# Attention's transposed probabilities returned in chunks of four key blocks, and each half's scores issued ahead of the other half's products with v

## The chip, the cores and the metric

The kernel runs on one core of a Trainium2 chip. The time is the device time of one launch in microseconds, as the median of several runs. TensorE (PE) multiplies matrices, with its weight loads shown apart (PEld); VectorE (DVE), ScalarE (ACT) and GpSimd (POOL) work on elements; SyncE (SP) issues all DMAs of this kernel in one queue, in order.

## The reference

One layer of a decoder on 2048 positions of width 1024, in float32: a mixer with three groups of heads (a Mamba-2 SSD, an RG-LRU and a forgetting attention), a SwiGLU feed-forward of width 2816, and a gated projection of a second input p, each added to the residual stream behind an RMS norm. The part that matters here is the forgetting attention: six heads of 64, in blocks of 128 queries.

```
cum = cumsum(log_f)
for blk in range(s // 128):
    logits = (q[blk] . k[:q1]) * scale + cum[queries] - cum[keys]
    probs = softmax(where(causal, logits, -inf))
    out[blk] = probs . v[:q1]
```

and behind it

```
h = h + concat[ssd, lru, fox] @ w_out
u = rmsnorm(h);  h = h + (silu(u @ w_gate) * (u @ w_up)) @ w_down
u = rmsnorm(h);  h = h + sigmoid(u @ w_ple_gate + b) * (p @ w_ple_proj)
```

## The kernel before

Activations lie transposed: 128 channels on the partitions, 512 positions (a block, four of them) in the free dimension. Every large product is made of float32r halves: a number is split into a rounded part and a rest, and three matmuls (high x high, high x low, low x high) are summed in PSUM. `mm3` (L194) makes one such product of a 128-column slab of weights: 8 x 3 matmuls of 512 columns. Its weights are loaded to `wst` (two buffers, L184), ScalarE copies the rounded part to `w` (three buffers, L190) and GpSimd subtracts it (L191).

The kernel has three phases. The first two make q, k, v, the recurrences and the SSD, and attention for block 0 (by another routine, `attention`). `phase3` (L802) then goes through the four blocks: gate and up products in three groups of hidden slabs with the down products behind each group (`FSPLIT`), then the projection of p and its gate, then `finish`, and in between the mixing product (`mix`, `load_y`) of the next block.

While block tb runs its feed-forward, attention for block tb + 1 runs at the side: `attention_t` (L692) is a Python generator, and `Side.tick` (L55) draws from it. Each `mm3` adds `rate` to a credit, and each whole credit runs the generator to its next `yield`. The rate is set so that all yields of a block are spent over RATE = 45 products. A last call, `side.finish()` in `load_y`, draws whatever is left, ahead of the norm of attention's output (L784 to L788).

This fixes the order in which the program is traced. A planner then takes all traced instructions, gives each the priority of its place in the program, and writes each engine's queue in a simulation of its own: an engine takes the first instruction in program order that the simulation believes ready, so a later one can be put ahead of an earlier one that waits. On the chip each engine works through its written queue in order, and semaphores hold it where data or buffers are late.

In `attention_t` for block qc there are K = 4 (qc + 1) key blocks, six heads, and per head two halves of 256 queries, hv = 1 and hv = 0. Per head k goes to `kx`, the forget bias to `cum`, q to `qx` and `qh`, v to `vc`, each with one buffer. For each 128-query block of a half, four score matmul pairs (L730, L731) are made, one per group of 32 keys out of each key block, with a yield behind each; VectorE adds the bias and takes the maximum (L732, into `lg`, two buffers); ScalarE takes the exponential with its sum (L738) and scales (L741); VectorE transposes squares of 32 x 32 (L742). Four DMAs write the result to a DRAM scratch `dp` (L746), and one reads it back with keys on the partitions into `pT` (L747). `pT` holds both query blocks of a half over all its key blocks, and has one buffer. When both are there (four empty yields, GAP, stand in between), `pT` is split into halves `ph` (two buffers): ScalarE copies the rounded part (L757), VectorE or GpSimd in turn subtracts (L758), and two matmuls per key block multiply with v into the PSUM bank `xd` (L761, L762), with a yield per key block. A copy (L765), an addition and a DMA to `dy` end the half.

The tags `kx`, `pT` and `lg` are used again behind attention: `px` (the split p, L843 to L848, from two loads of `in_pt` through the three `ld` buffers) takes `kx`, and `em` (eight tiles of projected p, later the block's result) takes `pT` and one of the two buffers of `lg`.

Of the kernel before, what the change touches and what calls it, by code (L numbers as in the profile page):

```python
# [11 lines left out]
F32 = mybir.dt.float32  # L12
F32R = mybir.dt.float32r
ACT = mybir.ActivationFunctionType
ALU = mybir.AluOpType
AX = mybir.AxisListType
# [3 lines left out]
P = 128  # L20
# [3 lines left out]
TB = 512  # L24
NTB = T // TB
NCH = TB // P
DFF = 2816
NF = DFF // P
# [1 line left out]
EPS = 1e-6  # L30
MASK = -1e30
RATE = 45
GAP = 4


PC = {}
# [29 lines left out]
class Trunk:  # L66
# [625 lines left out]
    def attention_t(self, qc, pool, tags, tag_o):  # L692


        nc = self.nc
        K = (qc + 1) * NCH
        tsl = slice(qc * TB, (qc + 1) * TB)
        banks = cycle(tags)
        HQ = 2 * P
        for h in range(6):  # L700
            kx = self.t(pool, [P, K, 4, 32], "kx", F32R)
            cum = self.t(pool, [P, 4, K, 32], "cum")
            qx = self.t(pool, [P, TB], "qx", F32R)
            qh = self.t(pool, [P, TB], "qh", F32R)
            o = slice(64 * (h % 2), 64 * (h % 2) + 64)
            q, k = self.dq[h // 2, o, :, tsl], self.dk[h // 2, o, :, 0:K * P]
            for s in range(2):
                nc.sync.dma_start(qx[64 * s:64 * s + 64].bitcast(F32), q[:, s])
                nc.sync.dma_start(kx[64 - 64 * s:128 - 64 * s].bitcast(F32).rearrange("p a g i -> p (a g i)"), k[:, s])
            for s in range(2):  # L710
                nc.sync.dma_start(qh[64 - 64 * s:128 - 64 * s].bitcast(F32), q[:, s])
            nc.sync.dma_start(cum.rearrange("p g k i -> p g (k i)"), self.dcug[h, :, 0:K].rearrange("g k i -> g (k i)").partition_broadcast(P))
            vc = self.t(pool, [P, K, P], "vc", F32R)
            for i in range(qc + 1):
                nc.sync.dma_start(vc[:, i * NCH:(i + 1) * NCH].bitcast(F32),
                                  self.dv[i * NCH:(i + 1) * NCH, :, h * P:(h + 1) * P].rearrange("t p c -> p t c"))
            for hv in (1, 0):
                KH = qc * NCH + 2 * hv + 2
                pT = self.t(pool, [P, 8, KH, 32], "pT")
                for qi in (2 * hv + 1, 2 * hv):  # L720
                    kv = qc * NCH + qi + 1
                    w = 32 * kv

                    nc.gpsimd.tensor_tensor(cum[:, :, kv - 1], cum[:, :, kv - 1], self.maskT.rearrange("p (g i) -> p g i", g=4), op=ALU.add)
                    lg = self.t(pool, [P, 4 * w], "lg", bufs=2)
                    mx = self.t(pool, [P, 4], "mx", bufs=2)
                    for g in range(4):
                        ps = self.ps(next(banks))[:, :w]
                        p3 = ps.rearrange("p (k i) -> p k i", i=32)
                        nc.tensor.matmul(p3, lhsT=qx[:, qi * P:(qi + 1) * P], rhs=kx[:, 0:kv, g], start=True, stop=False)  # L730
                        nc.tensor.matmul(p3, lhsT=qh[:, qi * P:(qi + 1) * P], rhs=kx[:, 0:kv, g], start=False, stop=True)  # L731
                        nc.vector.tensor_tensor_reduce(out=lg[:, g * w:(g + 1) * w], in0=ps, in1=cum[:, g, 0:kv].rearrange("p k i -> p (k i)"),  # L732
                                                       scale=1.0, scalar=-3e38, op0=ALU.add, op1=ALU.max, accum_out=mx[:, g:g + 1])
                        yield
                    m = self.t(pool, [P, 1], "m", bufs=2)
                    nc.vector.tensor_reduce(out=m, in_=mx, axis=AX.X, op=ALU.max, negate=True)  # L736
                    l = self.t(pool, [P, 1], "l", bufs=2)
                    nc.scalar.activation(lg, lg, ACT.Exp, bias=m, scale=1.0, accum_out=l)  # L738
                    r = self.t(pool, [P, 1], "r", bufs=2)
                    nc.vector.reciprocal(r, l)  # L740
                    nc.scalar.activation(lg, lg, ACT.Copy, scale=r)  # L741
                    nc.vector.transpose(lg, lg)  # L742
                    q0 = 4 * (qi - 2 * hv)
                    dp = self.t(self.dpool, [4, 32, 4, w], "dp", bufs=3)
                    for a in range(4):
                        nc.sync.dma_start(dp[:, :, a].rearrange("g i r -> i g r"), lg[32 * a:32 * a + 32].rearrange("p (g r) -> p g r", g=4))  # L746
                    nc.sync.dma_start(pT[:, q0:q0 + 4, 0:kv].rearrange("p a k j -> p a (k j)"), dp.rearrange("g i a r -> (g i) a r"))  # L747
                for _ in range(GAP):
                    yield
                po = self.ps(tag_o)[:, :HQ]  # L750
                for t0 in range(0, KH, 2):
                    ph = self.t(pool, [P, 2, 2, HQ], "ph", F32R, bufs=2)
                    spans = ((0, 2, 0),) if t0 + 2 < KH else ((0, 1, 0), (1, 2, 4))
                    for n, (i, j, d) in enumerate(spans):
                        src = pT[:, d:, t0 + i:t0 + j].rearrange("p a k j -> p k a j")
                        hi, lo = (ph[:, x, i:j, 32 * d:].rearrange("p k (a j) -> p k a j", j=32) for x in range(2))
                        nc.scalar.activation(hi, src, ACT.Copy)  # L757
                        (nc.vector if t0 % 4 == 0 else nc.gpsimd).tensor_tensor(lo, src, hi.bitcast(F32), op=ALU.subtract)  # L758
                    for i in range(2):
                        sl = slice(P if t0 + i == KH - 1 else 0, HQ)  # L760
                        nc.tensor.matmul(po[:, sl], lhsT=vc[:, t0 + i], rhs=ph[:, 0, i, sl], start=t0 + i == 0, stop=False)  # L761
                        nc.tensor.matmul(po[:, sl], lhsT=vc[:, t0 + i], rhs=ph[:, 1, i, sl], start=False, stop=t0 + i == KH - 1)  # L762
                        yield
                ot = self.t(self.tmp, [P, TB], "sq", bufs=3)[0:64, :HQ]
                nc.scalar.activation(ot, po[64:128], ACT.Copy)  # L765
                nc.vector.tensor_tensor(ot, po[0:64], ot, op=ALU.add)
                nc.sync.dma_start(self.dy[5 + h // 2, 64 * (h % 2):64 * (h % 2) + 64, qc * TB + HQ * hv:qc * TB + HQ * hv + HQ], ot)
                yield


    def load(self, src):
# [30 lines left out]
    def phase3(self, ctx):  # L802
        nc, tc, a = self.nc, self.tc, self.a
        pool = lambda name, bufs, **kw: ctx.enter_context(tc.tile_pool(name=name, bufs=bufs, **kw))
        one = pool("m4one", 1)
# [6 lines left out]
        h, u = self.first  # L812
        for tb in range(NTB):
            tsl = slice(tb * TB, (tb + 1) * TB)
            more = tb + 1 < NTB
            rate = 0
            if more:
                side.start(self.attention_t(tb + 1, one, ("xa", "xe", "xb", "xc"), "xd"))

                rate = 6 * (2 * (8 + GAP + 1) + 8 * (tb + 1) + 6) / RATE  # L820
            for f0, f1 in zip(FSPLIT[:-1], FSPLIT[1:]):
                hid = []
                for f in range(f0, f1):
# [12 lines left out]
                    hid.append(hh)  # L836
                if f1 == NF and more:
                    yx = self.load_y(tb + 1)
                for c in range(KD):
                    ps = self.mm3(self.weight(a["w_down"][c, :, f0:f1], f1 - f0), hid, rate)  # L840
                    nc.vector.tensor_tensor(h[c], h[c], ps, op=ALU.add)  # L841

            px = self.t(one, [P, 4, TB], "kx", F32R)  # L843
            px = [px[:, 0:2], px[:, 2:4]]
            for k in range(2):
                y = self.load(a["pt"][k, :, tsl])
                nc.scalar.activation(px[k][:, 0], y, ACT.Copy)
                nc.vector.tensor_tensor(px[k][:, 1], y, px[k][:, 0].bitcast(F32), op=ALU.subtract)  # L848
            em = []
            for tag, bufs in (("pT", None), ("lg", 2)):  # L850
                e = self.t(one, [P, 4, TB], tag, bufs=bufs)
                em += [e[:, i] for i in range(4)]
            for c in range(KD):
                if c % 4 == 0:
                    w = self.weight(a["w_pp"][c // 4], KD)
                if c == 2:
                    u = self.norm_split(h, "g3", eng=V, tag="xe")
                ps = self.mm3(w[:, :, 2 * (c % 4):2 * (c % 4) + 2], px)
# [7 lines left out]
            for c, cs in order:  # L866
# [14 lines left out]
                if not more:  # L881
                    sq = self.t(self.tmp, [P, TB], "sq", bufs=3) if acc is not None else self.t(self.tmp, [P, TB], "ssq", bufs=1)
# [7 lines left out]
            if more:  # L890
                h, u = hn, un
# [100 lines left out]
```

## Time and profile before

| | us |
|---|---|
| median of 3 runs | 2881.58 (2879.35 to 2887.67) |
| the profiled execution | 2888.08 |
| its span | 2886.3 |
| TensorE busy in it | 2753.8 |
| VectorE, ScalarE, GpSimd busy | 1633.1, 1297.9, 1398.3 |
| granted TensorE clock, mean | 0.979 |

Rows of the profile read as follows. A row of waits says who waited, for whom, the time in all, how often, and the longest. A row of a stretch gives its ends, its length, the busy time and number of instructions of PE, PEld, DVE, ACT and POOL, the granted clock, the mean busy share of the 16 DMA engines, and GB/s. A row of a tile or line gives the engine and operation, the count, the shortest, median and longest duration in ns, and the start of the first and the last. A row of DMA issues gives the count, the size of one and the median time from issue to landing. A row of the timeline or the chain gives start, length and what ran. Names such as `pT<-dp` are what is written and what is read.

### The profile page before, as it was taken

Reading aid. Unit: us, or ns where it says so; the run is one execution under the profiler, and the core shown is the slowest. Engines: PE = TensorE matmul, PEld = TensorE weight load, DVE = VectorE, ACT = ScalarE, POOL = GpSimd, SP = SyncE. Lnnn points to the kernel's source line nnn. Section 1 sums busy time; section 2 is a strip of 40 time slices with the busy share of each in tenths; the row PEclk is TensorE's granted clock in tenths of the full one; section 3 lists DMA queues with packets and bytes.
Section 4 is the critical chain, followed back from the end, with each engine's and each line's share of the span. In section 5 each row is a group of like instructions: output and inputs, shape, how many; then the busy total and the mean of one; then the engine's idle time right before and its main releaser. Section 6 shows DMA issues by size and latency. Waiting matters only on the chain.

```text
span 2886.3 us, 35956 instructions
## 1 busy us (share of the span) xinstructions
PE 2753.8 (95%) x12845; PEld 2286.2 (79%) x12845; DVE 1633.1 (57%) x2740; ACT 1297.9 (45%) x1977; POOL 1398.3 (48%) x985
## 2 busy tenths in 40 slices
PE   7999999998999999999999999999999989999997
PEld 5877777887877778888787888888878868888886
DVE  6887546767554543547565546566575454523246
ACT  4555535553353443434555534356564443322234
POOL 5334666655444444444454644444455534444443
PEclk8999999998999999999999999999999989999999
DMA  5544544452466554443877734268886532322231
GB/s 190 183 171 142 179 156 136 146 163 100 138 198 185 183 158 146 133 134 130 258 237 236 232 117 154 96 227 259 261 264 206 172 106 102 128 98 93 101 99 66
DMA packets 229644, 467.88 MB, mean 162 GB/s; under 512 B 24244, under 2 KB 118484, under 8 KB 227156
## 3 DMA queue, kind: packets, MB, share of 16 engines
q1 hardware_dynamic: 229466, 465.59, 50.4%
q8 instruction: 102, 1.67, 0.2%
q14 instruction: 76, 0.62, 0.1%
HBM read 371.62 MB, written 93.88 MB: 161 GB/s over the span
## 4 chain that ended last, share of the span: by engine, by line
PE 58%; DMA 14%; DVE 12%; ACT 6%; issue 4%; POOL 3%; SPq 3%; DVEq 0%; ACTq 0%; POOLq 0%
PE mm L200 17%; PE mm L202 16%; PE mm L201 16%; DMA dp<-lg 4%; DMA pT<-dp 2%; SPq L746 1%; ACT w L190 1%; DVE lg L742 1%; DVE u L227 1%; POOL w L191 1%; DMA kx<-dk 1%; PE xd L762 1%; DVE lg L732 1%; DMA wst<-in_w_up 1%; PE mm L218 1%
## 5 line engine op out<-in xcount | busy, mean ns | idle before, releaser
L191 POOL TENSOR_TENSOR w<-wst,w 128x1024 fp32r<-128x1024 f32 (+1 forms) x424 | 1015.8, 2398 | 962.9 <-ACT w L190 898.6
L200 PE MATMUL mm<-u,w 128*128 128x512 f32 (+1 forms) x3080 | 1207.6, 392 | 11.3 <-DVE h L488 5.4
L201 PE MATMUL mm<-u,w 128*128 128x512 f32 (+1 forms) x3080 | 1204.3, 391 | 1.9 <-DVE u L835 1.8
L202 PE MATMUL mm<-u,w 128*128 128x512 f32 (+1 forms) x3080 | 1204.1, 392 | 0.5 <-POOL w L191 0.5
L200 PEld LDWEIGHTS mm<-u,w 128*128 128x128 f32 x3080 | 582.3, 189 | 124.2 <-ACT w L190 5.2
L202 PEld LDWEIGHTS mm<-u,w 128*128 128x128 f32 x3080 | 582.0, 189 | 116.4 <-POOL w L191 2.1
L201 PEld LDWEIGHTS mm<-u,w 128*128 128x128 f32 x3080 | 582.0, 189 | 112.2 <-DVE u L835 2.6
L190 ACT ACTIVATE w<-wst 128x1024 fp32r<-128x1024 f32 (+1 forms) x424 | 440.2, 1039 | 483.2 <-PE mm L202 336.0
L758 DVE TENSOR_TENSOR ph<-pT,ph 128x512 fp32r<-128x512 f32 (+2 forms) x126 | 133.8, 1072 | 168.6 <-ACT ph L757 168.0
L758 POOL TENSOR_TENSOR ph<-pT,ph 128x512 fp32r<-128x512 f32 (+2 forms) x108 | 124.8, 1162 | 190.8 <-ACT ph L757 182.2
L835 DVE SCALAR_TENSOR_TENSOR u<-th,u 128x512 fp32r<-128x512 f32 x88 | 174.8, 1986 | 63.5 <-ACT u L834 63.2
L757 ACT ACTIVATE ph<-pT 128x512 fp32r<-128x512 f32 (+2 forms) x234 | 116.6, 539 | 193.5 <-DMA pT<-dp 142.7
L166 DVE TENSOR_TENSOR ssq<-ssq,sq 128x512 f32<-128x512 f32 x125 | 148.6, 1189 | 59.0 <-ACT sq L162 56.1
L738 ACT ACTIVATE lg<-lg,m 128x1024 f32<-128x1024 f32 (+5 forms) x72 | 102.0, 1417 | 99.4 <-DVE m L736 93.4
L742 DVE STREAM_TRANSPOSE lg<-lg 128x1024 f32<-128x1024 f32 (+5 forms) x72 | 113.5, 1577 | 47.9 <-ACT lg L741 47.8
L832 DVE TENSOR_TENSOR th<-th,mm 128x512 f32<-128x512 f32 x88 | 60.0, 681 | 141.6 <-PE mm L202 140.9
L841 DVE TENSOR_TENSOR h<-h,mm 128x512 f32<-128x512 f32 x96 | 65.2, 681 | 113.5 <-PE mm L202 113.3
L830 ACT ACTIVATE th<-mm 128x512 f32<-128x512 f32 x88 | 52.3, 595 | 168.2 <-PE mm L202 166.6
L761 PE MATMUL xd<-ph,vc 128*128 128x256 f32 (+1 forms) x396 | 107.1, 283 | 16.9 <-ACT ph L757 15.5
L831 DVE SCALAR_TENSOR_TENSOR th<-th,mm 128x512 f32<-128x512 f32 x88 | 60.1, 682 | 98.1 <-ACT th L830 98.1
L762 PE MATMUL xd<-ph,vc 128*128 128x256 f32 (+1 forms) x396 | 104.0, 291 | 8.9 <-DVE ph L758 8.1
L741 ACT ACTIVATE lg<-lg,r 128x1024 f32<-128x1024 f32 (+5 forms) x72 | 101.6, 1412 | 9.5 <-DVE r L740 9.4
(327 smaller groups left out, 3340.9 us busy)
## 6 DMA issues: line engine op xcount, KB each, us to landing
wst<-in_w_gate SPq DMA_DIRECT2D x88, 512.0 KB, 3.6
wst<-in_w_up SPq DMA_DIRECT2D x88, 512.0 KB, 3.5
wst<-in_w_down SPq DMA_DIRECT2D x64, 448.0 KB, 3.8
wst<-in_w_out SPq DMA_DIRECT2D x32, 512.0 KB, 3.5
wst<-in_w_down SPq DMA_DIRECT2D x32, 512.0 KB, 3.9
wst<-in_w_pg SPq DMA_DIRECT2D x32, 512.0 KB, 3.5
vc<-dv SPq DMA_DIRECT2D x60, 256.0 KB, 5.6
wst<-in_w_xbc SPq DMA_DIRECT2D x28, 512.0 KB, 4.1
```

Source lines behind the costliest of these rows:

```text
L166: (eng or nc.gpsimd).tensor_tensor(acc, acc, s, op=ALU.add)
L190: nc.scalar.activation(w[:, 0], st, ACT.Copy)
L191: nc.gpsimd.tensor_tensor(w[:, 1], st, w[:, 0].bitcast(F32), op=ALU.subtract)
L200: nc.tensor.matmul(ps, lhsT=w[:, 0, k], rhs=x[:, 0], start=k == 0, stop=False)
L201: nc.tensor.matmul(ps, lhsT=w[:, 0, k], rhs=x[:, 1], start=False, stop=False)
L202: nc.tensor.matmul(ps, lhsT=w[:, 1, k], rhs=x[:, 0], start=False, stop=k == len(u) - 1)
L742: nc.vector.transpose(lg, lg)
L757: nc.scalar.activation(hi, src, ACT.Copy)
L758: (nc.vector if t0 % 4 == 0 else nc.gpsimd).tensor_tensor(lo, src, hi.bitcast(F32), op=ALU.subtract)
L761: nc.tensor.matmul(po[:, sl], lhsT=vc[:, t0 + i], rhs=ph[:, 0, i, sl], start=t0 + i == 0, stop=False)
L762: nc.tensor.matmul(po[:, sl], lhsT=vc[:, t0 + i], rhs=ph[:, 1, i, sl], start=False, stop=t0 + i == KH - 1)
L835: nc.vector.scalar_tensor_tensor(hh[:, 1], th, 0.5, hh[:, 0].bitcast(F32), op0=ALU.mult, op1=ALU.subtract)
```

## The change

`attention_t` is cut into `load_keys`, `load_values`, `scores(h, hv)` and `outputs(h, hv)`. The halves are run in the order scores(0), then for each further half its scores and then the outputs of the half in front of it, and at the end the outputs of the last one. The keys are loaded with the scores of a head's first half, the values with its outputs. GAP is gone, and is gone from the rate. `dp` holds a whole half, and `pT` is read from it in chunks of four key blocks, each by two DMAs (one per query block), with three chunk buffers. In `phase3` the split p is made ahead of the last group of down products, and `em` takes both buffers of `lg`.

```diff
-        for h in range(6):
...
-            for hv in (1, 0):
-                KH = qc * NCH + 2 * hv + 2
-                pT = self.t(pool, [P, 8, KH, 32], "pT")
...
-                    dp = self.t(self.dpool, [4, 32, 4, w], "dp", bufs=3)
-                    for a in range(4):
-                        nc.sync.dma_start(dp[:, :, a].rearrange("g i r -> i g r"), lg[32 * a:32 * a + 32].rearrange("p (g r) -> p g r", g=4))
-                    nc.sync.dma_start(pT[:, q0:q0 + 4, 0:kv].rearrange("p a k j -> p a (k j)"), dp.rearrange("g i a r -> (g i) a r"))
-                for _ in range(GAP):
-                    yield
+        def scores(h, hv):
+            if hv:
+                load_keys(h)
+            kx, cum, qx, qh = keys[h]
+            dp = self.t(self.dpool, [4, 32, 8, qc * NCH + 2 * hv + 2, 32], "dp", bufs=3)
+            for qi in (2 * hv + 1, 2 * hv):
...
+                for a in range(4):
+                    nc.sync.dma_start(dp[:, :, 4 * (qi - 2 * hv) + a, 0:kv].rearrange("g i k j -> i g (k j)"),
+                                      lg[32 * a:32 * a + 32].rearrange("p (g r) -> p g r", g=4))
+            moved[h, hv] = dp
+
+        def outputs(h, hv):
+            if hv:
+                load_values(h)
+            vc, dp = vals[h], moved.pop((h, hv)).rearrange("g i a k j -> (g i) a k j")
+            KH = qc * NCH + 2 * hv + 2
+            po = self.ps(tag_o)[:, :HQ]
+            for t0 in range(0, KH, 2):
+                if t0 % 4 == 0:
+                    n = min(4, KH - t0)
+                    pT = self.t(pool, [P, 8, 4, 32], "pT", bufs=3)
+                    for a in range(2):
+                        e = n if a or t0 + n < KH else n - 1
+                        nc.sync.dma_start(pT[:, 4 * a:4 * a + 4, 0:e].rearrange("p a k j -> p a (k j)"),
+                                          dp[:, 4 * a:4 * a + 4, t0:t0 + e].rearrange("p a k j -> p a (k j)"))
...
+        halves = [(h, hv) for h in range(6) for hv in (1, 0)]
+        for i, half in enumerate(halves):
+            yield from scores(*half)
+            if i:
+                yield from outputs(*halves[i - 1])
+        yield from outputs(*halves[-1])
...
-                rate = 6 * (2 * (8 + GAP + 1) + 8 * (tb + 1) + 6) / RATE
+                rate = 6 * (2 * (8 + 1) + 8 * (tb + 1) + 6) / RATE
...
                 if f1 == NF and more:
                     yx = self.load_y(tb + 1)
+                if f1 == NF:
+                    px = self.t(one, [P, 4, TB], "kx", F32R)
+                    px = [px[:, 0:2], px[:, 2:4]]
+                    for k in range(2):
+                        y = self.load(a["pt"][k, :, tsl])
+                        nc.scalar.activation(px[k][:, 0], y, ACT.Copy)
+                        nc.vector.tensor_tensor(px[k][:, 1], y, px[k][:, 0].bitcast(F32), op=ALU.subtract)
                 for c in range(KD):
                     ps = self.mm3(self.weight(a["w_down"][c, :, f0:f1], f1 - f0), hid, rate)
                     nc.vector.tensor_tensor(h[c], h[c], ps, op=ALU.add)
...
-            for tag, bufs in (("pT", None), ("lg", 2)):
-                e = self.t(one, [P, 4, TB], tag, bufs=bufs)
+            for _ in range(2):
+                e = self.t(one, [P, 4, TB], "lg", bufs=2)
                 em += [e[:, i] for i in range(4)]
```

More of the change, by code (lines that the diff above doesn't have):

```diff
@@ L32 @@
 RATE = 45
-GAP = 4
 PC = {}
@@ L699, in attention_t, with load_keys @@
         HQ = 2 * P
-        for h in range(6):
+        keys, vals, moved = {}, {}, {}
+        def load_keys(h):
             kx = self.t(pool, [P, K, 4, 32], "kx", F32R)
@@ L712, in attention_t, with load_values @@
             nc.sync.dma_start(cum.rearrange("p g k i -> p g (k i)"), self.dcug[h, :, 0:K].rearrange("g k i -> g (k i)").partition_broadcast(P))
+            keys[h] = kx, cum, qx, qh
+        def load_values(h):
             vc = self.t(pool, [P, K, P], "vc", F32R)
@@ L716, in attention_t @@
                                   self.dv[i * NCH:(i + 1) * NCH, :, h * P:(h + 1) * P].rearrange("t p c -> p t c"))
-            for hv in (1, 0):
-                KH = qc * NCH + 2 * hv + 2
-                pT = self.t(pool, [P, 8, KH, 32], "pT")
[L720 to L733, printed above, removed]
-                        yield
[L735 to L743, printed above, removed]
-                    dp = self.t(self.dpool, [4, 32, 4, w], "dp", bufs=3)
-                    for a in range(4):
-                        nc.sync.dma_start(dp[:, :, a].rearrange("g i r -> i g r"), lg[32 * a:32 * a + 32].rearrange("p (g r) -> p g r", g=4))
-                    nc.sync.dma_start(pT[:, q0:q0 + 4, 0:kv].rearrange("p a k j -> p a (k j)"), dp.rearrange("g i a r -> (g i) a r"))
-                for _ in range(GAP):
-                    yield
[L750 to L768, printed above, removed]
@@ new lines, in load_values @@
+            vals[h] = vc
+        def scores(h, hv):
[4 more added lines that the diff above has]
+            for qi in (2 * hv + 1, 2 * hv):
+                kv = qc * NCH + qi + 1
+                w = 32 * kv
+                nc.gpsimd.tensor_tensor(cum[:, :, kv - 1], cum[:, :, kv - 1], self.maskT.rearrange("p (g i) -> p g i", g=4), op=ALU.add)
+                lg = self.t(pool, [P, 4 * w], "lg", bufs=2)
+                mx = self.t(pool, [P, 4], "mx", bufs=2)
+                for g in range(4):
+                    ps = self.ps(next(banks))[:, :w]
+                    p3 = ps.rearrange("p (k i) -> p k i", i=32)
+                    nc.tensor.matmul(p3, lhsT=qx[:, qi * P:(qi + 1) * P], rhs=kx[:, 0:kv, g], start=True, stop=False)
+                    nc.tensor.matmul(p3, lhsT=qh[:, qi * P:(qi + 1) * P], rhs=kx[:, 0:kv, g], start=False, stop=True)
+                    nc.vector.tensor_tensor_reduce(out=lg[:, g * w:(g + 1) * w], in0=ps, in1=cum[:, g, 0:kv].rearrange("p k i -> p (k i)"),
+                                                   scale=1.0, scalar=-3e38, op0=ALU.add, op1=ALU.max, accum_out=mx[:, g:g + 1])
+                    yield
+                m = self.t(pool, [P, 1], "m", bufs=2)
+                nc.vector.tensor_reduce(out=m, in_=mx, axis=AX.X, op=ALU.max, negate=True)
+                l = self.t(pool, [P, 1], "l", bufs=2)
+                nc.scalar.activation(lg, lg, ACT.Exp, bias=m, scale=1.0, accum_out=l)
+                r = self.t(pool, [P, 1], "r", bufs=2)
+                nc.vector.reciprocal(r, l)
+                nc.scalar.activation(lg, lg, ACT.Copy, scale=r)
+                nc.vector.transpose(lg, lg)
+                for a in range(4):
+                    nc.sync.dma_start(dp[:, :, 4 * (qi - 2 * hv) + a, 0:kv].rearrange("g i k j -> i g (k j)"),
+                                      lg[32 * a:32 * a + 32].rearrange("p (g r) -> p g r", g=4))
+            moved[h, hv] = dp
@@ new lines, in outputs @@
+        def outputs(h, hv):
[12 more added lines that the diff above has]
+                                          dp[:, 4 * a:4 * a + 4, t0:t0 + e].rearrange("p a k j -> p a (k j)"))
+                ph = self.t(pool, [P, 2, 2, HQ], "ph", F32R, bufs=2)
+                spans = ((0, 2, 0),) if t0 + 2 < KH else ((0, 1, 0), (1, 2, 4))
+                for i, j, d in spans:
+                    src = pT[:, d:, t0 % 4 + i:t0 % 4 + j].rearrange("p a k j -> p k a j")
+                    hi, lo = (ph[:, x, i:j, 32 * d:].rearrange("p k (a j) -> p k a j", j=32) for x in range(2))
+                    nc.scalar.activation(hi, src, ACT.Copy)
+                    (nc.vector if t0 % 4 == 0 else nc.gpsimd).tensor_tensor(lo, src, hi.bitcast(F32), op=ALU.subtract)
+                for i in range(2):
+                    sl = slice(P if t0 + i == KH - 1 else 0, HQ)
+                    nc.tensor.matmul(po[:, sl], lhsT=vc[:, t0 + i], rhs=ph[:, 0, i, sl], start=t0 + i == 0, stop=False)
+                    nc.tensor.matmul(po[:, sl], lhsT=vc[:, t0 + i], rhs=ph[:, 1, i, sl], start=False, stop=t0 + i == KH - 1)
+                    yield
+            ot = self.t(self.tmp, [P, TB], "sq", bufs=3)[0:64, :HQ]
+            nc.scalar.activation(ot, po[64:128], ACT.Copy)
+            nc.vector.tensor_tensor(ot, po[0:64], ot, op=ALU.add)
+            nc.sync.dma_start(self.dy[5 + h // 2, 64 * (h % 2):64 * (h % 2) + 64, qc * TB + HQ * hv:qc * TB + HQ * hv + HQ], ot)
+            yield
@@ L841, in phase3 @@
                     nc.vector.tensor_tensor(h[c], h[c], ps, op=ALU.add)
[L843 to L848, printed above, removed]
             em = []
-            for tag, bufs in (("pT", None), ("lg", 2)):
-                e = self.t(one, [P, 4, TB], tag, bufs=bufs)
+            for _ in range(2):
+                e = self.t(one, [P, 4, TB], "lg", bufs=2)
                 em += [e[:, i] for i in range(4)]
```

## The prediction

> **What bounds the kernel now.** I read the page first, then busy time by stage, then TensorE's waits stage by stage, the waits on the tile pT, and the chain of waits at two places.
>
> ```profile
> span 2886.3 us, 35956 instructions
> PE 2753.8 (95%) x12845; PEld 2286.2 (79%) x12845; DVE 1633.1 (57%) x2740; ACT 1297.9 (45%) x1977; POOL 1398.3 (48%) x985
> ```
>
> TensorE is busy for 95% of the span. The change adds and removes no matmul, so only TensorE's gaps, and the lower clock behind them, can be won. The third phase by stage (stretch in us, length, busy us and instructions of PE, PEld, DVE, ACT, POOL, granted clock, DMA share, GB/s):
>
> ```profile
> 792.00:1080.00 288.00, 267.72 (x1273) 220.56 (x1272) 142.69 (x345) 125.72 (x196) 128.39 (x87) 0.96 0.61 183
> 1368.00:1656.00 288.00, 277.56 (x1362) 232.70 (x1361) 165.42 (x346) 154.58 (x217) 144.70 (x98) 0.99 0.79 242
> 1872.00:2304.00 432.00, 421.85 (x1987) 351.34 (x1986) 265.05 (x432) 233.48 (x299) 217.03 (x133) 0.99 0.73 231
> 2304.00:2376.00 72.00, 58.51 (x258) 47.55 (x257) 37.20 (x58) 31.24 (x50) 26.40 (x14) 0.88 0.30 101
> 2376.00:2808.00 432.00, 431.70 (x1911) 356.94 (x1910) 167.58 (x166) 127.77 (x163) 194.34 (x83) 1.00 0.31 104
> ```
>
> The last row is feed-forward without attention: no gap, 432 us / 1911 = 226 ns per matmul of 512 columns, so 24 of them (one product, as I call it) take 5.4 us. The first three rows are attention for block 1, 2 and 3 (qc): idle 20.3, 10.4 and 10.2 us. The fourth is the end of attention for block 3: 13.5 us idle, clock 0.88. Who ended the idle time, in the same four stretches, in order:
>
> ```profile
> PE xd L761 <- ACT ph L757: 12.6, 7, 5.0
> PE xd L762 <- DVE ph L758: 4.8, 4, 2.1
> PE xd L761 <- DMA vc<-dv: 1.3, 1, 1.3
> ...
> PE xa L730 <- DMA kx<-dk: 3.9, 2, 2.4
> PE xd L761 <- ACT ph L757: 2.4, 2, 1.5
> PE xd L762 <- DVE ph L758: 1.3, 1, 1.3
> ...
> PE xa L730 <- DMA kx<-dk: 4.2, 2, 2.4
> PE xd L762 <- DVE ph L758: 1.9, 3, 1.0
> ...
> PE mm L200 <- ACT kx L847: 6.8, 1, 6.8
> PE xd L154 <- DVE sq L152: 3.7, 1, 3.7
> PE xd L140 <- DVE ssq L166: 3.0, 1, 3.0
> ```
>
> Two things can be won. In block 1 the products with v wait for the split probabilities (17.4 us). At the end, attention for block 3 is late and the norm (L140, L154) and the projection of p (L847) are exposed, 13.5 us.
>
> Behind the first stand the returning probabilities, for which ScalarE waits:
>
> ```profile
> L747 SPq DMA_DIRECT2D pT<-dp x72: 319/552/1954, 809.9 to 2290.4; - x72
> ...
>   ACT ph L757: 142.7, 34
> ...
> 809.94 0.36 DVE lg L732
> ...
> 812.19 5.62 DMA dp<-lg
> ...
> 823.33 0.61 ACT ph L757
> ```
>
> The last three rows are the chain at the first half of block 1: the write out, then the load back, then the split. They also show that VectorE takes the scores of the second half (L732 at 809.9) ahead of the first half's split at 823.3: the planner already runs scores ahead where it can.
>
> Behind the second: pT is one buffer, so the next half's load waits until this half's last split.
>
> ```profile
> L742 DVE STREAM_TRANSPOSE lg<-lg x72: 845/1576/2315, 803.3 to 2184.3; 128x1024 f32<-128x1024 f32 x6, 128x896 f32<-128x896 f32 x6, 128x768 f32<-128x768 f32 x6, 128x640 f32<-128x640 f32 x6
> ...
> L765 ACT ACTIVATE sq<-xd x36: 359/381/383, 834.5 to 2321.1; 64x256 f32<-64x256 f32 x36
> ...
> 2231.90 0.94 SPq L747 DMA_DIRECT2D pT<-dp  x2
> ...
> 2239.91 1.15 ACT L757 ACTIVATE ph<-pT 128x512 fp32r<-128x512 f32 x2 [0.60 <-DMA pT<-dp]
> ```
>
> The last scores are transposed at 2184, the last output is copied at 2321: the outputs lag by 137 us, and each half has a hole of 8.0 us (load at 2231.9, split at 2239.9).
>
> **The change part by part.** *pT in three chunk buffers.* Loads of the next chunks, of the next half too, go while this half is split, so the 8.0 us hole closes. Four halves or so remain after 2184; without their holes attention ends about 32 us sooner, near 2290. The chain behind its last output, from the write to the projection of p, has to move by only the 13.5 us that it is exposed now:
>
> ```profile
> 2322.42 1.95 DMA dy<-sq
> ...
> 2338.34 2.93 DMA ld<-in_pt
> 2341.29 0.64 ACT kx L847
> ```
>
> Worth: 13.5 us of idle time; the clock row adds at most 0.12 x 72 = 8.6. I take 3 of that, as part of the slow time was idle anyway, and keep 1.5 us for small waits: **15 us**, between 0 and 22.
>
> *Scores of half i+1 ahead of the products of half i; GAP goes.* In trace order the products came 4 yields after their scores, now 8. Yields per product fall with GAP from 5.33, 6.40, 7.47 to 4.27, 5.33, 6.40 for blocks 1 to 3, so 0.75, 0.63, 0.54 products become 1.9, 1.5, 1.25: at 5.4 us, 6.1, 4.7 and 3.9 us more slack. The longest wait is 5.0 us. But the planner had reordered already, and it issues at the time it believes the data ready; slack helps only where program order, not readiness, decides. I take half of the waits on ph in blocks 1, 2 and 3, 8.7 + 1.9 + 1.0, and 3 us of block 1's clock loss (0.04 x 288 = 11.5): **14.6 us**, between 0 and 34.5 (all 23.0 and all the clock). The last pair of halves of a block has no scores behind it and gains nothing.
>
> *DMAs.* A half's two pT loads become two per chunk: 4, 6 and 8 per half for blocks 1, 2, 3, so 216 issues for 72. The nearest row to a chunk load is the load of v, as large and in the same runs of 512 bytes:
>
> ```profile
> vc<-dv SPq DMA_DIRECT2D x60, 256.0 KB, 5.6
> ...
> qx<-dq SPq DMA_DIRECT2D x48, 128.0 KB, 3.7
> ...
> cum<-dcug SPq DMA_DIRECT2D x6, 1024.0 KB
> kx<-dk SPq DMA_DIRECT2D x12, 512.0 KB, 9.2
> pT<-dp SPq DMA_DIRECT2D x6, 1024.0 KB, 6.6
> ...
> pT<-dp SPq DMA_DIRECT2D x6, 832.0 KB, 7.4
> ...
> SPq L184 <- POOL w L191: 1280.4, 314, 17.4
> ```
>
> 144 more issues at the 552 ns of L747 are 79 us of SP over 1000 us, under the 1280 us in which SP only waits for a weight buffer to come free. Behind a pT load that waits for its buffer stand the weight loads. They have two staging buffers and three split ones ahead of TensorE: some 16 us of cover, so I take 0. If that cover goes, it is the slower rival below.
> The Trainium skill says (DMA: Bandwidth & Descriptors, section Bandwidth) that DMAs should be batched to 1 MiB and more for 75% of peak, which speaks against pieces of 256 KB; with the 2.0 us fixed and 436 GB/s of its section Anatomy of one DMA, eight pieces one after another are an estimated 21 us, the two loads of today 9: 12 us lost per half of block 3, 144 us over its twelve, and 2998 for 2855 if nothing of it were hidden. The trace agrees in part: 256 KB land in 5.6 us and 1024 KB in 6.6; but the pieces are asked for a chunk and more ahead, and their times overlap.
>
> *v a half later.* The v buffer comes free after the last half of the head before; its load now has 8 yields instead of 12. The row above has one wait of 1.3; I charge two such, 2.6 us, between 0 and 18 heads x 1.3 = 23.
>
> *Order unchanged for k.* kx still has one buffer; the waits on it (3.9 and 4.2 us) stay.
>
> *Projection of p ahead of the last down products; its sums in both lg buffers.* Two loads, two copies and two subtractions move ahead of eight down products; they lie on ScalarE and VectorE, busy 45% and 57%, cost 0. The next block's first scores now find both lg buffers held until the result is written. Before, their last group came behind that scaling anyway (groups end at 1354.9, scaling of lg at 1347.0 to 1349.7), so a few us of attention's start, under feed-forward: 0, bound 5.
>
> ```profile
> 1347.02 2.71 DVE L906 SCALAR_TENSOR_TENSOR lg<-lg,par,xb 128x512 f32<-128x512 f32 x4
> ...
> 1354.91 0.55 DVE L732 CUSTOM_DVE_ANT_0 lg<-xb,cum 128x384 f32<-128x384 f32 x1
> ```
>
> **Sum.** 15 + 14.6 - 2.6 = 27 us. The profiled execution took 2888.1 us (span 2886.3), 6.5 above the median 2881.6; 2861.1 for a like one, **2854.6** as a median.
>
> **Rivals.** *Only the end is won:* the planner already had the scores ahead, and places each product where it believes it ready, so first products wait as now: 2881.6 - 15 + 2.6 = 2869.
> *Nearly all is won:* waits on ph and the whole end, 34.5 + 22 = 56.5: 2825.
> *Nothing moves:* the outputs keep their pace because the two ph buffers and the split, not the load, set it (loads at 2231.9 and, two halves on, 2290.4: 29 us a half, of which the hole is 8); attention still ends near 2320, and block 1's waits move to the next chunk: 2881, within 8.
> *Slower, by block 3's transfers:* today the lag spreads them.
>
> ```profile
> 2088.00:2160.00 72.00, 69.24 (x327) 56.51 (x326) 51.57 (x90) 44.62 (x55) 35.87 (x25) 1.00 0.85 266
> ```
>
> That is the highest rate of any such stretch. A half needs half of a head's k, cum, q and v (two of 512, 1024, four of 128 and four of 256 KB: 1792 KB for the half) and its probabilities, two loads of 1024 to 832 KB, 1856 KB on the mean, written and read: 5504 KB, 5.6 MB. The program order asks for 45 products in 12 halves: 20.3 us, and 0.52 MB of weights each, 2.0 MB. Attention's own matmuls (16 of up to 512 columns and 60 of 256) are 7 us by the 226 ns. So 7.6 MB in 27.3 us, 278 GB/s. At 266 a half takes 1.3 us longer, 16 us over 12 halves; at 231, the mean of block 3 now, 5.6, 67 us. TensorE waits for that in order if the planner believed in more. I take 29, nearer to the 266 of the same work; less the 13.6 won in blocks 1 and 2: 2897. It decides from the point where the DMAs cannot hold 278 GB/s. For it: share 0.85 already. Against: 15% is left, and the waits on kx are few. The batching rule of the Trainium skill, quoted above, makes this the case to expect, as the smaller pieces would lower the rate.
>
> **How the numbers follow.** Chances: forecast 0.42 (own range 2838 to 2866), only the end 0.17, nearly all 0.11, nothing 0.12, slower 0.18. Three runs spread by 0.3%, which is what can be told from no change (8.6 us). Faster by more: 0.42 + 0.17 + 0.11 less a little for the edges, 0.68; within 0.13; slower 0.19. The range 2818 to 2894 leaves out about two thirds of the slower case and the far end of the nearly-all case.
>
> **What would show it.** In the changed profile: ScalarE's wait on pT<-dp under 70 us of 142.7; the last output of block 3 copied 30 us and more sooner, beyond what was won ahead of it; the wait on L847's place gone and clock 1.00 there; waits on ph in block 1 near 9 us; kx waits still near 8; 216 pT issues. Wrong if DMA share in block 3 is above 0.9 with waits on kx, vc or weights that were not there, or if outputs still trail the scores by 100 us.

## The result, and the profile after

The changed kernel takes 2863.79 us (median of 5, 2855.48 to 2867.89) against 2881.58 (2879.35 to 2892.92): a ratio of 0.9926, interval 0.99 to 0.9952. That is 17.8 us, where 27 were forecast. The profiled execution took 2864.66 us, 23.4 less than the one of before: the latter was 6.5 us above its median, the former 0.9.

Busy time by stage of the changed kernel, same stretches as before (ends, length, PE, PEld, DVE, ACT, POOL, granted clock, DMA share, GB/s), and one stretch inside block 3:

```profile
792.00:1080.00 288.00, 277.21 (x1362) 231.53 (x1361) 144.68 (x363) 134.49 (x209) 139.57 (x93) 0.99 0.68 198
...
1368.00:1656.00 288.00, 271.53 (x1317) 227.27 (x1316) 164.84 (x323) 146.29 (x209) 143.09 (x95) 0.98 0.80 230
...
1872.00:2304.00 432.00, 421.55 (x2000) 350.20 (x1999) 266.02 (x438) 232.19 (x299) 222.24 (x136) 0.99 0.80 232
2304.00:2376.00 72.00, 70.36 (x312) 57.32 (x311) 47.37 (x51) 32.51 (x46) 32.66 (x14) 1.00 0.39 132
...
1932.00:2004.00 72.00, 68.66 (x322) 57.32 (x321) 51.18 (x100) 44.25 (x52) 36.98 (x26) 0.95 0.97 291
```

Block 1 (first row) has 89 matmuls more in the same 288 us and a clock of 0.99 for 0.96; the end of block 3 (fourth row) is full, clock 1.00 for 0.88. Block 2 (second row) is worse than before: 16.5 us idle for 10.4. TensorE's waits in the four stretches, in order:

```profile
PE xd L780 <- ACT ph L776: 5.3, 2, 4.3
PE xd L780 <- DMA vc<-dv: 3.5, 1, 3.5
...
PE xd L781 <- DVE ph L777: 0.9, 1, 0.9
...
PE xa L739 <- DMA kx<-dk: 5.4, 1, 5.4
PE xa L739 <- DMA pT<-dp: 3.3, 1, 3.3
PE xd L781 <- DVE ph L777: 2.5, 4, 0.9
PE xd L781 <- POOL ph L777: 2.0, 1, 2.0
...
PE xa L739 <- issue: 3.1, 2, 1.9
PE xa L739 <- DMA kx<-dk: 2.7, 1, 2.7
...
PE mm L199 <- ACT lg L886: 1.4, 1, 1.4
```

In block 1 the waits on ph fell from 17.4 to 6.2 us. The wait on the split of p, and those of the norm in front of it, are gone; the 1.4 us in the last row is for the projected p's copy. In block 2 the scores (L739) wait for k. The 3.3 us that are put down to a load of pT are most likely k's too: scores do not read pT, and the wait ended at 1449.6, six us after k's second load had been issued, behind four writes to dp:

```profile
1441.28 2.14 SPq L753 DMA_DIRECT2D dp<-lg  x4
1443.47 0.85 SPq L711 DMA_DIRECT2D kx<-dk  x1
```

The loads of pT, what waits for them, the last transposes and output copies:

```profile
L769 SPq DMA_DIRECT2D pT<-dp x216: 359/500/4582, 809.1 to 2264.9; - x108
...
  ACT ph L776: 49.5, 13
...
L751 DVE STREAM_TRANSPOSE lg<-lg x72: 830/1571/2312, 802.4 to 2163.8; 128x1024 f32<-128x1024 f32 x6, 128x896 f32<-128x896 f32 x6, 128x768 f32<-128x768 f32 x6, 128x640 f32<-128x640 f32 x6
...
L784 ACT ACTIVATE sq<-xd x36: 362/381/383, 834.2 to 2286.5; 64x256 f32<-64x256 f32 x36
```

There are 216 loads for 72. ScalarE waits 49.5 us for them, 142.7 before. The last output of block 3 is copied at 2286.5, 34.6 us sooner.

For what follows I use one measure of my own: the distances between the starts of successive matmuls, less 0.443 ns per column (227 ns for 512 columns) and at least 108 ns, as close as they stand where nothing waits, summed. It counts idle time and slow clock together, as time that TensorE lost; the stretches run from the first scores of a block (a few that run far ahead of the rest are left out) to its last output, and the fourth is the 70 us behind block 3's. Ratios are to the kernel before on the same chip. The ratio is from all executions of a kernel, the four columns from its one profiled execution; executions of one kernel differ by up to 17 us here, and two pairs that have the same attention code (before and p moved alone, changed and p moved back) differ by up to 4 us in a column.

| kernel | ratio (95% interval) | block 1 | block 2 | block 3 | end |
|---|---|---|---|---|---|
| before | 1 | 38.8 | 21.6 | 25.2 | 17.9 |
| changed | 0.9926 (0.99 to 0.9952) | 20.9 | 32.8 | 24.4 | 2.7 |
| p moved back | 0.9908 (0.9892 to 0.9923) | 23.3 | 28.8 | 23.0 | 2.9 |
| p moved alone | 0.9991 (0.9978 to 1.0004) | 36.5 | 20.6 | 25.9 | 16.5 |
| chunks alone | 0.996 (0.9945 to 0.9975) | 35.1 | 34.1 | 26.1 | 1.1 |
| order alone | 0.9991 (0.998 to 1.0002) | 23.7 | 34.7 | 28.2 | 18.0 |
| k, bias, q doubled | 0.987 (0.9855 to 0.9884) | 21.9 | 20.4 | 24.7 | 2.9 |
| k, q doubled | 0.9911 (0.9897 to 0.9924) | 21.8 | 20.3 | 29.6 | 2.8 |
| chunks of eight | 0.9924 (0.9909 to 0.9939) | 28.2 | 20.8 | 24.9 | 4.9 |
| one chunk buffer | 1.0072 (1.0058 to 1.0086) | 16.4 | 33.0 | 48.7 | 18.1 |
| over 44 products | 0.9911 (0.9895 to 0.9927) | 18.0 | 22.4 | 33.4 | 6.1 |
| over 46 products | 0.9891 (0.9877 to 0.9906) | 19.4 | 23.8 | 30.1 | 2.7 |
| k doubled, three lg | 0.9866 (0.985 to 0.9883) | 17.2 | 22.0 | 23.2 | 5.5 |

The four columns fell by 22.7 us from before to changed; the two spans differ by 23.7. So the table holds nearly all of the change: 17.9 won in block 1, 15.2 at the end, 0.8 in block 3, 11.2 lost in block 2.

### The profile page after: what moved, and what is told of

It reads as the page before. It is cut to its first block, busy times and chain, and to the rows that moved or that the text cites. A ratio compares the mean times of both kernels' runs of the same rounds, so it can differ in the third digit from the quotient of the medians.

```text
span 2862.6 us, 36351 instructions
## 1 busy us (share of the span) xinstructions
PE 2745.4 (96%) x12845; PEld 2280.4 (80%) x12845; DVE 1636.1 (57%) x2740; ACT 1297.6 (45%) x1977; POOL 1407.3 (49%) x985
## 4 chain that ended last, share of the span: by engine, by line
PE 65%; DMA 10%; DVE 9%; ACT 4%; POOL 4%; issue 4%; SPq 3%; DVEq 0%; POOLq 0%; ACTq 0%
PE mm L199 18%; PE mm L201 18%; PE mm L200 18%; DMA dp<-lg 2%; POOL w L190 2%; DMA kx<-dk 1%; DMA pT<-dp 1%; PE xd L781 1%; PE xd L780 1%; DMA cum<-dcug 1%; PE mm L217 1%; DMA ld<-dy 1%; PE mm L212 1%; SPq L753 1%; PE mm L213 1%
```

## Experiments: which part won what

Three theories. 1: the chunk buffers win the end, the order wins block 1. 2: the planner had the scores ahead already and the chunks win both. 3: the move of p wins the end.

**p moved back.** The changed kernel with the block of `px` behind the down products again:

```diff
-                if f1 == NF:
-                    px = ...
                 for c in range(KD):
                     ps = self.mm3(self.weight(a["w_down"][c, :, f0:f1], f1 - f0), hid, rate)
...
+            px = ...
```

> The changed kernel with one step undone: the split of p is made behind the last down products again. Theory 1 (the chunk buffers end attention for block 3 sooner, and that alone covers what stands behind it): the end stays won, TensorE's idle time in the last stretch of block 3 stays under 3 us, 2864 us within 6. Theory 3 (the move of p is what covered the end): the wait on the split of p comes back with some 7 us and its clock, 2872 us or more.

2860.33 us, 0.9908: within the interval of the changed kernel, end 2.9 us. Theory 3 falls: where attention ends in time, the move of p is worth nothing.

**p moved alone**, on the kernel before (the same edit the other way):

```diff
+                if f1 == NF:
+                    px = ...
                 for c in range(KD):
...
-            px = ...
```

> The kernel before with the move of p alone. Theory 1: nothing, 2881 us within 5, because the loads of p need the buffers that the late norm of attention's output holds. Theory 3: 7 to 15 us faster, 2867 to 2875 us, and the wait on the split of p gone.

0.9991, no difference that can be told. The row at the end of block 3 is that of before, to 0.2 us:

```profile
PE mm L200 <- ACT kx L844: 7.0, 1, 7.0
```

**Chunks alone**, on the kernel before; order, GAP and rate stay, and the projected p takes both lg buffers as in the change:

```diff
-                pT = self.t(pool, [P, 8, KH, 32], "pT")
+                dp = self.t(self.dpool, [4, 32, 8, KH, 32], "dp", bufs=3)
...
+                    if t0 % 4 == 0:
+                        pT = self.t(pool, [P, 8, 4, 32], "pT", bufs=3)
+                        (two loads, as in the change)
```

> The kernel before with the chunks alone (DRAM scratch of a whole half, three chunk buffers, both lg buffers for the projected p); the order of scores and products, GAP, the rate and the place of p stay. Theory 1: the last output of block 3 some 25 to 35 us sooner and the end won, 15 us, 2866 us; waits on ph in block 1 stay near 17 us. Theory 2 (the planner had the scores ahead already, the chunks carry everything): the waits in block 1 fall as in the changed kernel too, 2855 to 2864 us.

0.996, 11 us. The end is won (1.1 us lost for 17.9), and block 1 keeps its waits on ph, as theory 1 has it and theory 2 not:

```profile
PE xd L767 <- ACT ph L763: 10.1, 6, 4.0
PE xd L768 <- DVE ph L764: 7.4, 5, 1.9
```

The gain is 4 us short of the 15 of theory 1: block 2 lost 12.5 us more than before, which no theory had.

**Order alone**, with one pT for a whole half and p in its old place:

```diff
+            pT = self.t(pool, [P, 8, KH, 32], "pT")
+            for a in (1, 0):
+                e = KH + a - 1
+                nc.sync.dma_start(pT[:, 4 * a:4 * a + 4, 0:e]..., dp[:, 4 * a:4 * a + 4, 0:e]...)
             for t0 in range(0, KH, 2):
-                if t0 % 4 == 0:
-                    ...
```

> The changed order alone (scores of a half ahead of the products of the half in front, no GAP, the rate that goes with it), with one pT buffer for a whole half, loaded by two DMAs when its products are due, and p in its old place. Theory 1: block 1's waits on ph fall from 17 to about 6 us with their clock, 12 to 20 us won; the end stays late and costs its 13.5 us: 2862 to 2869 us. Theory 2: no gain, 2881 us or more, as the single pT buffer still makes each half wait for its load.

0.9991: no gain in the time, so theory 1 missed the total, and the total is what theory 2 had named. By stage theory 1 is right on block 1 and on the end, and theory 2, by which block 1 wins nothing here, is not. Block 1 lost 23.7 us for 38.8 (the forecast 12 to 20 won), and the end kept its waits:

```profile
PE mm L199 <- ACT kx L871: 6.8, 1, 6.8
PE xd L153 <- DVE sq L151: 3.7, 1, 3.7
PE xd L139 <- DVE ssq L165: 3.1, 1, 3.1
```

Block 2 again lost 13.1 us more and block 3 another 3.0, as much as was won. (The profiled execution was the slowest of twelve, 7.8 us above their median, so these losses may be too large by some us.) So order and chunks each win what theory 1 says, in a stage of its own, and the two gains add up (block 1: 15.1 and 3.7, together 17.9; end: 0 and 16.8, together 15.2). The loss in block 2 comes with either and does not add up: 12.5 and 13.1, together 11.2.

**One chunk buffer** for three:

```diff
-                    pT = self.t(pool, [P, 8, 4, 32], "pT", bufs=3)
+                    pT = self.t(pool, [P, 8, 4, 32], "pT", bufs=1)
```

> The changed kernel with one chunk buffer in place of three. If the number of buffers (loads ahead of the split) closes the hole between halves: the hole comes back, now at every chunk, block 3's attention ends later than before the change, and the end costs its 15 us or more: 2885 us or more, 0.998 to 1.01. If the smaller first piece alone does it: within 4 us of the changed kernel.

1.0072: slower than the kernel before, as the first reading has it. It is the buffers, not the small first piece. ScalarE waits five times as long for the loads, the last output slips to 2334, and the end is exposed again:

```profile
  ACT ph L776: 245.8, 76
...
L784 ACT ACTIVATE sq<-xd x36: 362/382/385, 831.9 to 2334.3; 64x256 f32<-64x256 f32 x36
...
PE mm L199 <- ACT kx L870: 6.7, 1, 6.7
PE xd L139 <- DVE ssq L165: 4.4, 1, 4.4
PE xd L153 <- DVE sq L151: 2.4, 1, 2.4
```

Block 1, where a half has two chunks, was best of all with it (16.4 us): there the single buffer takes nothing away. Two or three buffers of a whole half were not tried.

## Experiments: what block 2 lost

Theory A: k, bias and q come late behind the probabilities in the one DMA queue. Theory B: the loss belongs to one written order, and any nudge redraws it. Theory C: small pieces cost.

**k, bias and q doubled**, chunk buffers from three to two to make room:

```diff
-            kx = self.t(pool, [P, K, 4, 32], "kx", F32R)
-            cum = self.t(pool, [P, 4, K, 32], "cum")
+            kx = self.t(pool, [P, K, 4, 32], "kx", F32R, bufs=2)
+            cum = self.t(pool, [P, 4, K, 32], "cum", bufs=2)
...
-                    pT = self.t(pool, [P, 8, 4, 32], "pT", bufs=3)
+                    pT = self.t(pool, [P, 8, 4, 32], "pT", bufs=2)
```

> The changed kernel with two buffers each for k, bias and q (kx, cum, qx, qh), so that the next head's loads need not wait for the last scores of the head before; the chunk buffers fall from three to two to make room. Theory A (block 2 lost what block 1 won because k, q and bias come late behind the probabilities in the one DMA queue): the waits of the scores fall from some 13 us to under 4 in block 2 and from 11 to under 4 in block 3, with their clock; 15 to 22 us faster than the changed kernel, a ratio of 0.985 to 0.988 to the kernel before. Theory B (block 2 loses because the planner's order is off by as much wherever something is ready late, whatever it is): the waits move to the products, less than 6 us are won, 0.990 or above.

2849.3 us, 0.987, faster than both kernels and in the range of theory A. In block 2 the loss fell to 20.4, as A says, and no score waits for a transfer any more; but the scores wait 6.3 us for PSUM banks, which VectorE empties, where A had named under 4. In block 3 A is wrong: the loss stayed (24.7), as all of the scores' wait moved there:

```profile
PE xa L739 <- DVE mx L741: 9.9, 5, 3.6
```

**k and q doubled**, bias not, three chunk buffers:

```diff
-            kx = self.t(pool, [P, K, 4, 32], "kx", F32R)
+            kx = self.t(pool, [P, K, 4, 32], "kx", F32R, bufs=2)
...
-            qx = self.t(pool, [P, TB], "qx", F32R)
-            qh = self.t(pool, [P, TB], "qh", F32R)
+            qx = self.t(pool, [P, TB], "qx", F32R, bufs=2)
+            qh = self.t(pool, [P, TB], "qh", F32R, bufs=2)
```

> The changed kernel with two buffers for k and q alone, three chunk buffers as in the change. Theory A: nearly as the run with bias doubled too, since TensorE itself reads only k and q: 0.986 to 0.989; if bias (which VectorE needs) is what is late behind them, the waits move to the PSUM banks of the scores (mx) and less than half is won. Theory B: 0.990 or above.

0.9911, outside the range of A and in that of B. Block 2 is as good (20.3), block 3 worse (29.6), and the path was only in part the one A named: the scores wait for PSUM banks (4.2 us in block 2, 3.1 in block 3), but the larger waits of block 3 are now the products':

```profile
PE xd L781 <- POOL ph L777: 5.4, 2, 4.5
PE xd L780 <- DMA vc<-dv: 4.1, 2, 3.5
PE xa L739 <- DVE mx L741: 3.1, 2, 1.8
```

**Chunks of eight key blocks** in two buffers, half the loads, runs of 1024 bytes:

```diff
-                if t0 % 4 == 0:
-                    n = min(4, KH - t0)
-                    pT = self.t(pool, [P, 8, 4, 32], "pT", bufs=3)
+                if t0 % 8 == 0:
+                    n = min(8, KH - t0)
+                    pT = self.t(pool, [P, 8, 8, 32], "pT", bufs=2)
```

> The changed kernel with chunks of eight key blocks in two buffers: half as many loads, twice the run length (1024 bytes). Theory C (small pieces cost: more packets and issues delay everything behind them): block 2 falls back to some 22 us of lost TensorE time, 8 to 12 us faster than the changed kernel, 0.987 to 0.989. Theories A and B: no gain, 0.991 to 0.995; the first product of a half comes later as its first piece is larger.

0.9924, as the changed kernel. Block 2 fell to 20.8, which is what theory C said; block 1 rose to 28.2. A half there is one chunk now: its products wait 8.0 us for ScalarE's split (5.3 in the changed kernel), and its scores 5.0 us for PSUM banks, where they had no such wait. In total larger pieces won nothing.

So two unlike edits, more buffers for k and q and larger chunks, had brought block 2 to 20 us. That speaks for theory B, which the next two test: number, size and buffers of the transfers stay, only the pace at which attention is drawn changes.

**Over 44 and over 46 products**, for 45 (in the second, 46 for 44):

```diff
-RATE = 45
+RATE = 44
```

> The changed kernel with attention spread over 44 products in place of 45, and nothing else. Theory A (k, q and bias come late in block 2 because of the change's transfers): the lost TensorE time of block 2 stays within 4 us of the changed kernel's 33, as the transfers are the same; time within 6 us of it. Theory B (block 2's loss is that of one written order, which any nudge redraws): block 2 changes by 6 us or more, most likely down to some 20 to 25 us, as in the runs with k doubled or larger chunks; 0.987 to 0.992.

> The changed kernel with attention spread over 46 products. Theory A: block 2's lost time within 4 us of 33, time within 6 us of the changed kernel. Theory B: block 2 changes by 6 us or more in either direction, and blocks 1 and 3 may too.

0.9911 and 0.9891, neither told apart from the changed kernel. Block 2 fell to 22.4 and 23.8, and block 3 rose to 33.4 and 30.1. Theory A's bound of 4 us is broken in both: how much block 2 loses depends on the written order, as theory B has it. The wait that A named did not go, though. Over 44 products the scores of block 2 still wait 6.5 us for transfers:

```profile
PE xa L739 <- DMA kx<-dk: 4.0, 1, 4.0
PE xa L739 <- DMA pT<-dp: 2.5, 1, 2.5
```

Over 46 they wait 7.6 us, in the changed kernel 8.7, before 4.7, and with k and q doubled not at all. What the other pace moved out of block 2 is the products' wait (4.5 us in the changed kernel, 1.6 and 2.0 here) and slow clock. Blocks 2 and 3 together lost 57.2 us in the changed kernel, 55.8 and 53.9 here, 51.8 with p moved back, 46.8 before. So in these four kernels the change costs some 5 to 10 us on the two blocks, and in which of them the cost falls is a matter of one written order. It is no fixed price: with chunks of eight the two lost 45.7.

**k doubled and three buffers for the scores:**

```diff
-            kx = self.t(pool, [P, K, 4, 32], "kx", F32R)
+            kx = self.t(pool, [P, K, 4, 32], "kx", F32R, bufs=2)
...
-                lg = self.t(pool, [P, 4 * w], "lg", bufs=2)
+                lg = self.t(pool, [P, 4 * w], "lg", bufs=3)
```

> The changed kernel with two buffers for k and three for the scores (lg). Where k, q and bias were all doubled, what was left of the scores' waits in blocks 2 and 3 was for PSUM banks, which VectorE frees late because it waits for a scores buffer whose write to DRAM has not landed. If so: the scores' waits on mx fall under 3 us in blocks 2 and 3, and with k doubled the time comes to 0.983 to 0.987 of the kernel before. If q or bias, which have one buffer here, are as late as k was: 0.989 to 0.992.

2853.34 us, 0.9866, in the range that was named: with k, bias and q doubled (0.987) the best here; the two are not told apart. In block 3 the wait on mx is down to 2.4 us, which fits a third buffer for the scores as the cure; in block 2 it is 3.6, above the 3 expected. What is left is spread over v and q:

```profile
PE xa L739 <- DVE mx L741: 3.6, 2, 2.0
...
PE xd L780 <- DMA vc<-dv: 3.5, 2, 2.2
PE xa L739 <- DVE mx L741: 2.4, 1, 2.4
PE xa L739 <- DMA qx<-dq: 2.2, 1, 2.2
```

Blocks 2 and 3 together lost 45.1 and 45.2 us in the two best kernels, below the 46.8 of before: second buffers for what the scores read take back what the change had cost there. They take away nearly all of the scores' waits for transfers in block 2, which the other pace did not; but the larger chunks reached the same sum without them, so how much of it is the earlier k and how much one more written order, these runs do not separate.

## Why the prediction was right, step by step

**The end, 15 us forecast:** 15.2 measured. It is the chunk buffers', shown by the runs with chunks alone, order alone and one buffer. But the working behind it was off. I had each of four last halves shorter by the whole hole of 8.0 us. From the copies of the output, the last four halves of block 3 take 26.1 us each (2182.3 to 2286.5), 28.5 before (2207.2 to 2321.1). Only 2.4 of the 8.0 were won there. The 8.0 us run from the issue of a load to the split; ScalarE itself stood idle for the load 2.8 us a half, in the last four halves before the change (2207 to 2322):

```profile
ACT ph L757 <- DMA pT<-dp: 11.2, 4, 3.7
```

In the last four halves of the changed kernel this wait is gone. My own row had said so: the split at 2239.91 waited 0.60 us for the load. The rest of the pace is set by other work, as the rival "nothing moves" had said. Block 3's attention, by the stretches of the table, still became 25.6 us shorter (424.0 for 449.6), most of it earlier in the block. My sign asked for 30, beyond what was won ahead. It needed only 13.5: the term had room to spare and came out right with half of its reason, which is luck as far as the 8.0 us go. My sign for a failure, outputs that trail the scores by 100 us, was a bad one: they trail by 122.7 (2163.8 to 2286.5, 137 before), and nothing waits for that.

**First products, 14.6 us forecast, 11.7 of it in block 1:** block 1 won 17.9. Waits on ph fell by 11.2 for the 8.7 forecast, and all idle time by 9.5, as waits on v grew; the other 8 or so came with the clock, 0.99 for 0.96, where I had taken 3. That the planner had reordered already did not spoil it: the run with the order alone won 15.1 there.

**Block 2, 1.9 won and k unchanged:** this is the step that failed. It lost 11.2 us more. The scores' wait for k went from 3.9 to 5.4 us, with the 3.3 that are put down to pT beside it, and those on ph from 3.7 to 4.5, where half of them were to go; idle time grew by 7.3 us in all, and slow clock makes up the rest. I had said that k's order stays, so its waits stay. The transfers in front of it did not stay, nor did the written order around it; how much each of the two does is open. Block 3's 1.0 came as 0.8: its waits on ph nearly went, but other waits took their place.

**v, 2.6 us charged:** the waits on v went from 1.3 to 3.5 in block 1 and 0.8 in block 3, 3.0 us more.

**The slower rival** was to decide at 278 GB/s in block 3, with 266 as the highest rate of before. That was read off stretches on a fixed grid. Between them the kernel before had already moved 290:

```profile
1962.00:2034.00 72.00, 67.44 (x304) 55.71 (x303) 44.29 (x89) 39.29 (x44) 29.89 (x20) 0.95 0.91 290
```

So 266 was no limit. (The count of 60 products of 256 columns per half is a slip for 30; its 7 us are those of 30.) Over block 3 the rate rose only from 225 to 233 GB/s, at a share of 0.80 for 0.72, and TensorE lost no more there than before (24.4 for 25.2 us). The sign that I had named against me came in part: a share of 0.97 for 72 us, in the row above, and a wait of 0.8 us on v that was not there; but the wait on k fell, from 4.2 to 2.7 us. Whether what TensorE waits for at such a share is bandwidth, no run here tells. By the Trainium skill (DMA: Bandwidth & Descriptors, section Bandwidth), larger pieces should have helped; its figures, and those of my estimate of 2998 us, are for DMAs that GpSimd issues, and these are SyncE's. The run with chunks twice as large agrees with it in block 2 alone and not in the total, 0.9924 for 0.9926.

**The move of p and the lg buffers, 0:** shown for p by two runs. The lg buffers were not tried by themselves.

**The sum:** 15.2 + 17.9 + 0.8 - 11.2 = 22.7 us in the profiled execution for 27 forecast, 17.8 between the medians; the missed term is block 2's. The 2863.79 us lie 9 us above the forecast and 5 below the rival "only the end", so the time alone does not tell the two apart: block 1 does, and it won 6 us more than its term, which hid half of what block 2 fell short.

## What to carry to other kernels

A buffer that is filled by a round trip through DRAM should be cut so that the next piece can be on its way while this one is used; the cut paid here through the number of buffers, not through the size of the pieces (more buffers of the whole size were not tried). Cost a change stage by stage: here two parts won in two different stages, and each took 12 to 13 us from a third, so that one of them, the order, moved the time by nothing when it was made alone. Where a planner writes the queues, a loss that a neutral nudge moves to another stage belongs to that order and not to the edit alone; test for it before explaining it, and look at the sum of the stages.

## What was not expected of the hardware

With the one queue of SyncE, in pieces of 64 to 1024 KB, the DMAs moved 291 GB/s over 72 us at a share of 0.97 in the changed kernel, and 290 at 0.91 before. TensorE was busy for 68.7 and 67.4 of these 72 us, at a clock of 0.95 in both: at this load it lost no more of its time after the change than before.
